# Folded router weights, ScalarE statistics, and the first layer's modulation steps ahead of its output projection

## The chip, the cores and the metric

The kernel runs on one core of one Trainium2 chip. The core has a matrix engine (TensorE, PE in the profile), VectorE (DVE), ScalarE (ACT), GpSimd (POOL) and SyncE (SP), which here only issues transfers; the engines run side by side, each through a queue of its own in order, and wait for one another by semaphores. The metric is the device time of one execution in microseconds (us), as the median of several runs.

## What is computed

Two layers over 256 latent tokens and 256 context tokens of width 1024. In each layer a modulation vector of 6 x 1024 numbers is computed for either kind of token, four mixers and a gated merge give the first update, a router and 16 experts the second. The output is the latent stream, so the second layer treats the context only as far as the latent tokens need it.

```python
def modulate(x, shift, scale):
    return layer_norm(x) * (1 + scale) + shift
...
for l in range(DEPTH):
    mod_lat = jnp.split((jax.nn.silu(c) @ w_mod[l] + b_mod[l])[:, None, :], 6, axis=-1)
    ...
    y_lat = token_mix_out(p_lat, o_lat, *mix_w)
    h_lat = affine_ln(DN_ALPHA * h_lat + mod_lat[2] * y_lat, ln1_g[l], ln1_b[l])
    m_lat = hier_moe(modulate(h_lat, mod_lat[3], mod_lat[4]), *moe_w)
    h_lat = affine_ln(DN_ALPHA * h_lat + mod_lat[5] * m_lat, ln2_g[l], ln2_b[l])
```

`token_mix_out` merges four branches (gated DeltaNet, conformer, Fourier, spatial gating unit), each by its projection and a sigmoid gate, and multiplies the sum with `w_out`. `hier_moe` computes 4 group logits and 16 expert logits per token (20 columns together), takes the best group, the best two of its four experts and weights for both, and adds up two gated MLPs with 512 hidden units.

## The kernel before

**Tiles.** Tokens lie in tiles of 128: layer 0 has four (0 and 1 latent, 2 and 3 context), layer 1 two. A large product is made in three matmuls on halves of each number (`mm3`): `split` turns a loaded weight tile `w` (128 x 512) into a high part `wh` on ScalarE and a low part `wl` on VectorE, and TensorE multiplies high by high, low by high and high by low into PSUM (`psmm`). The tiles rotate through rings of buffers, five of them named `w`. A weight is asked for on SyncE's queue, whose transfers start in order, each as soon as the buffer that it fills is free; GpSimd's queue carries token rows, the scratch tensor `h2s` and gathers.

**Order.** The functions emit the work, and a list scheduler then puts the instructions of each engine in an order by priorities and dependences. Program order is thus near the order of the code without being equal to it, and the instructions of one function can stand among those of another. An engine doesn't leave this order while it runs.

**Mixers and merges of a layer.** `conf_in`, `sgu` and `rms_z` project the normed input, and `merge` is called once for each mixer. It runs over eight output blocks `dt` of 128 channels: a gate projection, the branch's projection, the gated sum on VectorE, and `self.pump(1)` at the end unless the branch is the conformer's (i = 1).

**Modulation steps.** `mod_steps` is a generator over three banks b of a layer (shift and scale of the first norm; gate and shift; scale and gate, as 2 x 1024 numbers for each kind of token). A step asks SyncE for two tiles of 512 KB of `in_wmod_dram` into the ring `w` and multiplies them with the conditioning vectors `silc` into a PSUM bank `psg`; two or eight tiles of weights later `mod_rows` adds the bias, sends the rows to DRAM (`mods`), and transposes those of banks 0 and 1 into `modT`, so that they lie along the partitions. `pump(n)` takes n steps. In layer 0, 24 of 32 steps (banks 1 and 2 of layer 0, banks 0 and 2 of layer 1) are taken in `merge`; of the other eight, `mix_out` takes four, `moe` and later code the rest, with `pump(9)` at the start of `moe`.

**Output projection and its tail.** `mix_out` loads `h` (the residual), splits the merged tensor, and for each pair of tiles s runs `wout(s)`, eight blocks of `w_out`, whose result is scaled by the gate on ScalarE (`yT`). In `norms(tt)` TensorE transposes a tile's result back, VectorE adds it to the residual, takes the statistics (`bn_stats` on two halves, `bn_aggr`, a root on ScalarE, a reciprocal), and applies the first norm with two `scalar_tensor_tensor` operations, giving `h`; then it does the same once more with the modulation rows, giving `xm`, which GpSimd's queue writes to `h2s`. In `logits(tt)` TensorE transposes `xm`, ScalarE copies that to `h2Tt`, and 8 matmuls with the router weights `rw` give 20 columns of `plog` (in the trace each of these stands as two). `route` adds the bias and takes the group maximum `gmx`; a long chain of small VectorE operations follows (`route`, `rank`, up to `mxi`, the largest excess), from whose result the indices `ix` for the gather of the tokens of the first expert come. By "tail" the prediction means the stretch from the first sum of residual and projection to `gmx`. In layer 0 the pair of tiles 2 and 3 comes first (s = 1), then tiles 0 and 1.

## Time and profile before

| | |
|---|---|
| median of 3 runs (lowest, highest) | 1875.15 us (1873.21, 1880.23) |
| profiled execution: its own time, its span | 1878.1 us, 1876.3 us |
| TensorE busy | 1721.4 us, 92% |
| VectorE busy | 1208.7 us, 64% |
| ScalarE busy | 848.3 us, 45% |
| GpSimd busy | 222.4 us, 12% |
| mean granted clock of TensorE, as a share of full speed | 0.953 |
| moved by transfers | 396.50 MB, mean 211 GB/s |

The profile shows one execution. Its span runs from the first to the last instruction that it records, and the execution's own time is 1.8 us longer. The busy shares are means over the whole span; the granted clock is the rate at which TensorE was allowed to run, 1 standing for 2.4 GHz and 0.5 for 1.2 GHz.

### The profile page before, as it was taken

The numbers are of one execution on the slowest core, as the hardware profiler recorded it, in microseconds if no ns is written. First come the engines' busy times: TensorE is split into PE (matmuls) and PEld (weight loads), VectorE is DVE, ScalarE is ACT, GpSimd is POOL, SyncE is SP. The second block draws the span as 40 slices with busy tenths as digits, with TensorE's granted clock in tenths as the row PEclk, the third lists the DMA queues.
The fourth block names the chain that finished last, engine by engine and source line by source line (L and its number), as shares of the span: only waits on it lengthen the run. The fifth ranks groups of instructions, "written<-read, shape, count | busy, mean of one in ns | idle before, by whom it ended". The sixth has DMA issues, their size and how long they took to land. (4 is left out here: it accounts for less than half of the span.)

```text
span 1876.3 us, 31714 instructions
## 1 busy us (share of the span) xinstructions
PE 1721.4 (92%) x11399; PEld 1274.5 (68%) x11399; DVE 1208.7 (64%) x2631; ACT 848.3 (45%) x1688; POOL 222.4 (12%) x321
## 2 busy tenths in 40 slices
PE   7999999998999999699999959989998996799994
PEld 2777777786777788377666516787898996566541
DVE  5878597397353457698575487698678676556203
ACT  3544552343233345187565435445555562355211
POOL 1011101000000205111111021110010010111110
PEclk8999999999999999899999978999999997899997
DMA  8321004523535845889999882222144585799994
GB/s 333 98 75 46 13 24 161 193 88 123 172 125 189 315 144 187 293 309 397 388 379 382 328 309 71 73 82 67 46 136 148 167 318 187 290 414 411 403 410 159
DMA packets 112732, 396.50 MB, mean 211 GB/s; under 512 B 16256, under 2 KB 16352, under 8 KB 112560
## 3 DMA queue, kind: packets, MB, share of 16 engines
q1 hardware_dynamic: 99120, 359.87, 52.6%
q0 software_dynamic: 13440, 34.44, 5.2%
q8 instruction: 94, 1.54, 0.3%
q14 instruction: 78, 0.64, 0.1%
HBM read 388.43 MB, written 17.35 MB: 216 GB/s over the span
## 5 line engine op out<-in xcount | busy, mean ns | idle before, releaser
L266 ACT ACTIVATE wh<-w 128x512 fp32r<-128x512 f32 x500 | 310.1, 630 | 418.4 <-PE psmm L257 299.6
L263 DVE TENSOR_TENSOR wl<-w,wh 128x512 fp32r<-128x512 f32 x484 | 333.6, 701 | 190.1 <-ACT wh L266 184.2
L257 PE MATMUL psmm<-xh,wh 128*128 128x256 f32 (+1 forms) x1280 | 442.3, 346 | 1.2 <-ACT wh L266 1.2
L257 PE MATMUL psmm<-xh,wl 128*128 128x256 f32 (+1 forms) x1280 | 437.7, 342 | 3.9 <-POOL wl L263 3.0
L257 PE MATMUL psmm<-xl,wh 128*128 128x256 f32 (+1 forms) x1280 | 434.5, 340 | 2.2 <-DVE xl L263 2.2
L257 PEld LDWEIGHTS psmm<-xh,wh 128*128 128x128 f32 x1280 | 244.7, 191 | 52.5 <-issue 16.0
L257 PEld LDWEIGHTS psmm<-xh,wl 128*128 128x128 f32 x1280 | 244.3, 191 | 39.4 <-issue 6.5
L257 PEld LDWEIGHTS psmm<-xl,wh 128*128 128x128 f32 x1280 | 244.8, 191 | 31.0 <-issue 3.3
L977 DVE SCALAR_TENSOR_TENSOR cx<-cbuf,part,cx 128x512 f32<-128x512 f32 (+1 forms) x240 | 142.9, 613 | 2.1
L257 PE MATMUL psmm<-br,wh 128*128 128x512 f32 (+1 forms) x512 | 127.7, 336 | 0.4 <-ACT cth L266 0.4
L263 DVE TENSOR_TENSOR hid<-hid,psmm 128x256 f32<-128x256 f32 (+1 forms) x32 | 17.2, 537 | 136.1 <-PE psmm L257 121.2
L257 PEld LDWEIGHTS psmm<-br,wh 128*128 128x128 f32 x512 | 87.4, 188 | 11.7 <-ACT cth L266 0.6
L263 DVE TENSOR_TENSOR xh<-w,xh 128x512 fp32r<-128x512 f32 x124 | 80.7, 686 | 19.1 <-ACT xh L266 17.1
L257 PE MATMUL psmm<-br,wl 128*128 128x512 f32 (+1 forms) x256 | 86.5, 338 | 1.1 <-DVE wl L263 1.1
L257 PE MATMUL psmm<-xh,xTh 128*128 128x512 f32 x224 | 80.0, 415 | 5.7 <-ACT xh L266 5.1
L266 ACT ACTIVATE xh<-w 128x512 fp32r<-128x512 f32 x124 | 72.2, 627 | 19.7 <-DMA w<-in_expert_w_gate_dram 7.2
L257 PE MATMUL psg<-w,silc 128*32 128x512 f32 x320 | 64.5, 657 | 15.5 <-DMA w<-in_wmod_dram 15.5
L257 PE MATMUL psmm<-w,xTh 128*64 128x256 f32 x560 | 67.6, 387 | 1.6 <-DMA w<-in_expert_w_up_dram 1.1
L266 ACT ACTIVATE ye<-psmm,m 128x512 f32<-128x512 f32 x46 | 30.3, 684 | 72.7 <-PE psmm L257 72.3
L257 PEld LDWEIGHTS psmm<-w,xTh 128*64 128x64 f32 x560 | 41.0, 139 | 26.6 <-issue 5.1
L257 PEld LDWEIGHTS psmm<-xh,xTh 128*128 128x128 f32 x224 | 41.3, 190 | 24.6 <-ACT xh L266 9.7
L266 ACT ACTIVATE xTh<-psg 128x512 fp32r<-128x512 f32 (+1 forms) x46 | 26.3, 597 | 63.2 <-PE psg L260 61.5
(474 smaller groups left out, 2847.3 us busy)
## 6 DMA issues: line engine op xcount, KB each, us to landing
w<-in_wch_dram SPq DMA_DIRECT2D x136, 512.0 KB
w<-in_wmod_dram SPq DMA_DIRECT2D x80, 512.0 KB
w<-in_expert_w_down_dram SPq DMA_DIRECT2D x77, 512.0 KB
w<-in_expert_w_gate_dram SPq DMA_DIRECT2D x76, 512.0 KB
w<-in_expert_w_up_dram SPq DMA_DIRECT2D x71, 512.0 KB
w<-in_wbr_dram SPq DMA_DIRECT2D x32, 512.0 KB
xl<-in_expert_w_up_dram SPq DMA_DIRECT2D x28, 512.0 KB
xl<-in_expert_w_gate_dram SPq DMA_DIRECT2D x26, 512.0 KB
```

The source lines that it names most:

```text
L257: self.nc.tensor.matmul(out, lhsT, rhs, start=start, stop=stop, **k)
L263: (eng or self.nc.vector).tensor_tensor(out, a, b, op)
L266: self.nc.scalar.activation(out, in_, func, **k)
L977: nc.vector.scalar_tensor_tensor(x, w, dw[:, c, k:k + 1], x, op0=ALU.mult, op1=ALU.add)
```

## The change

Four edits go together.

- **Router fold.** The logits are no longer a product of the modulated token with the router weights. `router_fold` makes, for each kind of token, weights `scale * rw` with the mean over the 1024 inputs subtracted from each of the 20 columns, and a constant row `c` from the shift and the bias. Then `logits` transposes `h`, not `xm`, and a `scalar_tensor_tensor` on VectorE multiplies the result by the reciprocal deviation `rs` and adds `c`. The folds are made at `dt == 5` of the last gated merge that takes steps (i = 0). `mod_rows` transposes bank 2 as well, since the fold needs the scale along the partitions.
- **Statistics on ScalarE.** The last pair of tiles (0 and 1) goes through `norms_last`. Tile 0's first norm keeps `bn_stats`; tile 1's first norm and the second norm of both get their mean and squares from `norm_sums`, two ScalarE passes over 1024 columns that add up their elements. The rows `xm` are then made by `modulate`, beside the logits.
- **Steps.** `pump(1)` is added in `rms_z` (4 times), in `conf_in` for c > 1 (2) and in `sgu` (4), for layer 0 only. With the 24 of the merges that is more than the generator has, so all 32 steps are taken before `mix_out`, and the calls in `mix_out` and later find none.
- **Small ones.** The factor `ALPHA` of the residual moves into the scale of the projection and into the epsilon of the first norm (`epsa`), and a constant of the ranking is replaced by a comparison.

```diff
+    def norm_sums(self, src, u, eps, junk):
+        rs, st, nm = (self.sb([P, w], f"{n}{u}") for w, n in ((1, "lrs"), (4, "lst"), (2, "lnm")))
+        self.act(junk, src, AF.Identity, accum_out=st[:, 0:1])
+        self.act(nm[:, 1:2], st[:, 0:1], AF.Identity, scale=-1.0 / D)
+        self.act(junk, src, AF.Square, bias=nm[:, 1:2], accum_out=st[:, 2:3])
+        self.act(rs, st[:, 2:3], AF.Sqrt, bias=eps, scale=1.0 / D)
+        self.nc.vector.reciprocal(rs, rs)
+        return nm[:, 1:2], rs
...
     def mod_rows(self, l, b, hfs, rows, bm, pt, mt):
...
-        if b == 2:
-            return
...
-            for m in ((0, 1), (0,))[b]:
+            for m in ((0, 1), (0, 1), (0,))[b]:
...
     def rms_z(self, l, nt):
...
         for hd in range(4):
+            if l == 0:
+                self.pump(1)
...
     def conf_in(self, l, nt, cs):
...
         for c in cs:
+            if l == 0 and c > 1:
+                self.pump(1)
...
     def sgu(self, l, nt):
...
             u = gelu(c)
+            if l == 0:
+                self.pump(1)
...
     def merge(self, l, i, br, nt, first):
...
             if i != 1:
                 self.pump(1)
+            if i == 0 and dt == 5:
+                self.fold = {s: self.router_fold(l, s) for s in reversed(range(nt // 256))}
...
+    def router_fold(self, l, s):
...
+        self.tt(tv, rw, shift[:, :, None].to_broadcast([P, KD, 20]))
+        nc.vector.tensor_reduce(part[:, 0], tv.rearrange("p k n -> p n k"), AX.X, ALU.add)
+        self.tt(w, rw, scale[:, :, None].to_broadcast([P, KD, 20]))
+        nc.vector.tensor_reduce(part[:, 1], w.rearrange("p k n -> p n k"), AX.X, ALU.add)
+        pt = self.ps()
+        self.mm(pt[:, 0:40], self.ones, t[:, 160:200], True, True)
+        self.tt(c, pt[:, 0:20], self.rb, ALU.add)
+        nc.vector.scalar_tensor_tensor(w, pt[:, None, 20:40].to_broadcast([P, KD, 20]), -1.0 / D, w, op0=ALU.mult, op1=ALU.add)
+        return w, c
...
     def mix_out(self, l, ntt):
...
-                nc.vector.scalar_tensor_tensor(x[:, c], h1[:, c], ALPHA, pt, op0=ALU.mult, op1=ALU.add)
-            self.norm_affine(h1, x, g1, b1, f"a{tt % 2}")
+                self.tt(x[:, c], h1[:, c], pt, ALU.add)
...
+        def norms_last():
+            x0, x1 = self.sb([P, D], "xm"), self.sb([P, D], "xm")
...
+                    self.tt(x[:, c], self.h[:, tt, c], pt, ALU.add)
+            mu, rs = self.norm_stats(x0, "a0", self.epsa)
+            nm1, rs1 = self.norm_sums(x1, 0, self.epsa, self.h[:, 1])
+            nc.vector.scalar_tensor_tensor(x0, x0, mu, g1, op0=ALU.subtract, op1=ALU.mult)
+            nc.vector.scalar_tensor_tensor(self.h[:, 0], x0, rs, b1, op0=ALU.mult, op1=ALU.add)
+            nc.vector.scalar_tensor_tensor(x1, x1, nm1, g1, op0=ALU.add, op1=ALU.mult)
+            nc.vector.scalar_tensor_tensor(self.h[:, 1], x1, rs1, b1, op0=ALU.mult, op1=ALU.add)
+            return [(x, *self.norm_sums(self.h[:, tt], tt, self.eps, x), ALU.add) for tt, x in enumerate((x0, x1))]
...
-                    self.tr(pt[:, 128 * k:128 * k + 128], x[:, 512 * q + 128 * k:512 * q + 128 * k + 128])
+                    self.tr(pt[:, 128 * k:128 * k + 128], self.h[:, tt, 512 * q + 128 * k:512 * q + 128 * k + 128])
...
+            nc.vector.scalar_tensor_tensor(self.lg[:, tt], plog[:, 20 * tt:20 * tt + 20], rs, c, op0=ALU.mult, op1=ALU.add)
...
         for tt in range(2, ntt):
-            logits(tt, xs[tt])
+            logits(tt, xs[tt][2])
         self.pump(1)
-        logits(0, xs[0])
-        logits(1, xs[1])
+        for tt in (0, 1):
+            modulate(tt, *xs[tt])
+        for tt in (0, 1):
+            logits(tt, xs[tt][2])
         self.pump(3)
```

How the order of the instructions moves is shown at three places; the numbers behind the names tell one buffer from another.

**ScalarE, tail of layer 1.** `yT` is the scaled projection, `a0brs` to `b1brs` are roots for the two norms of tiles 0 and 1, `h2Tt` are copies for the router. Before, from the last copy of the projection but one:

```order
L266 ACTIVATE yT_17299<-psmm_17563,ys_3247_17288,ys_3246_17287 128x256
L266 ACT_TABLE_LOAD
L266 ACTIVATE a0brs_17604<-a0bag_17603,eps_69 128x1
L266 ACTIVATE a1brs_17638<-a1bag_17637,eps_69 128x1
L266 ACTIVATE b0brs_17614<-b0bag_17613,eps_69 128x1
L266 ACTIVATE h2Tt_17657<-psmm_17658 128x512
L266 ACTIVATE h2Tt_17657<-psmm_17664 128x512
L266 ACTIVATE b1brs_17648<-b1bag_17647,eps_69 128x1
```

After, up to the first such copy, `lst` and `lnm` being the sums and negated means of `norm_sums`:

```order
L265 ACTIVATE yT_17354<-psmm_17619,ys_3260_17343,ys_3259_17342 128x256
L265 ACTIVATE h_17321,lst_3326_17680<-xm_17646 128x1024
L265 ACTIVATE lnm_3327_17681<-lst_3326_17680 128x1
L265 ACTIVATE h_17321,lst_3326_17680<-xm_17646,lnm_3327_17681 128x1024
L265 ACT_TABLE_LOAD
L265 ACTIVATE a0brs_17673<-a0bag_17672,epsa_71 128x1
L265 ACTIVATE lrs_3325_17679<-lst_3326_17680,epsa_71 128x1
L265 ACTIVATE xm_17645,lst_3329_17692<-h_17321 128x1024
L265 ACTIVATE lnm_3330_17693<-lst_3329_17692 128x1
L265 ACTIVATE h2Tt_17713<-psmm_17714 128x512
```

Three passes over 1024 columns and two one-column operations now stand between the projection and the first copy for the router, and the table load stands behind the second of the passes.

**VectorE, tail of layer 1.** Before, from the second norm of tile 0 to that of tile 1:

```order
L448 SCALAR_TENSOR_TENSOR xm_17589<-h_17266,b0bag_17613,rowt_3251_17297 128x1024
L432 RECIPROCAL a1brs_17638<-a1brs_17638 128x1
L449 SCALAR_TENSOR_TENSOR xm_17589<-xm_17589,b0brs_17614,rowt_3250_17295 128x1024
L449 SCALAR_TENSOR_TENSOR h_17266<-xm_17623,a1brs_17638,rowt_3249_17293 128x1024
L428 BN_STATS b1bst_17646<-h_17266 128x6
L429 BN_STATS b1bst_17646<-h_17266 128x6
L430 BN_AGGR b1bag_17647<-b1bst_17646 128x2
L448 SCALAR_TENSOR_TENSOR xm_17623<-h_17266,b1bag_17647,rowt_3251_17297 128x1024
L432 RECIPROCAL b1brs_17648<-b1brs_17648 128x1
L449 SCALAR_TENSOR_TENSOR xm_17623<-xm_17623,b1brs_17648,rowt_3250_17295 128x1024
```

After, from the first norm of tile 1 to the second norm of both (`lg` are the logits):

```order
L1271 SCALAR_TENSOR_TENSOR xm_17646<-xm_17646,lnm_3327_17681,rowt_3261_17346 128x1024
L432 RECIPROCAL a0brs_17673<-a0brs_17673 128x1
L1270 SCALAR_TENSOR_TENSOR h_17321<-xm_17645,a0brs_17673,rowt_3262_17348 128x1024
L441 RECIPROCAL lrs_3325_17679<-lrs_3325_17679 128x1
L1272 SCALAR_TENSOR_TENSOR h_17321<-xm_17646,lrs_3325_17679,rowt_3262_17348 128x1024
L1277 SCALAR_TENSOR_TENSOR xm_17645<-h_17321,lnm_3330_17693,rowt_3264_17352 128x1024
L441 RECIPROCAL lrs_3328_17691<-lrs_3328_17691 128x1
L1278 SCALAR_TENSOR_TENSOR xm_17645<-xm_17645,lrs_3328_17691,rowt_3263_17350 128x1024
L1291 SCALAR_TENSOR_TENSOR lg_17356<-psg_17355,lrs_3328_17691,rwc_3127_16695 128x20
L1277 SCALAR_TENSOR_TENSOR xm_17646<-h_17321,lnm_3333_17701,rowt_3264_17352 128x1024
L441 RECIPROCAL lrs_3331_17699<-lrs_3331_17699 128x1
L1278 SCALAR_TENSOR_TENSOR xm_17646<-xm_17646,lrs_3331_17699,rowt_3263_17350 128x1024
```

The statistics of `h` by `bn_stats` are gone; the second norm's products of tile 0 are followed by its logits, and those of tile 1 stand behind them.

**TensorE, last part of the spatial gating unit of layer 0.** `wsT` are the gating weights, `vln` the normed values, `xh` and `wh` halves of the projection. Before, three tiles of modulation weights (`w`, `silc`) lie ahead of the first gating product:

```order
L257 MATMUL psmm_4084<-xh_137,wl_4081 128x512
L260 MATMUL psmm_4112<-ident_77,ca_4061 128x128 x4
L257 MATMUL psg_4235<-w_4236,silc_66 32x512 x2
L257 MATMUL psg_4235<-w_4238,silc_66 32x512 x2
L257 MATMUL psg_4235<-w_4303,silc_66 32x512 x2
L257 MATMUL psmm_4136<-wsT_3697,vln_4111 128x128
```

After, from the second tile ahead of the transposes of `ca`:

```order
L256 MATMUL psmm_4142<-xh_139,wl_4139 128x512
L256 MATMUL psg_3558<-w_4169,silc_66 32x512 x2
L256 MATMUL psg_3558<-w_4171,silc_66 32x512 x2
L259 MATMUL psmm_4178<-ident_79,ca_4119 128x128 x4
L256 MATMUL psg_3558<-w_4288,silc_66 32x512 x2
L256 MATMUL psg_3558<-w_4290,silc_66 32x512 x2
L256 MATMUL psmm_4202<-wsT_3731,vln_4177 128x128
```

Two steps (four tiles) now stand about the transposes, two tiles ahead of them and two behind.

## Rows read from the trace of the kernel before

**Rows 1.** Busy time by stretch: stretch, its length, then by engine, clock, DMA share.

```profile
290.00:690.00 400.00, 392.73 (x1804) 300.20 (x1803) 222.22 (x404) 134.98 (x230) 28.90 (x39) 0.99 0.51 173
748.00:777.00 29.00, 26.14 (x170) 15.02 (x168) 19.99 (x37) 7.26 (x16) 1.11 (x2) 0.94 0.94 341
794.00:1087.00 293.00, 280.34 (x1440) 189.96 (x1440) 200.54 (x418) 183.65 (x329) 37.73 (x42) 0.97 0.94 360
1566.00:1589.20 23.20, 11.68 (x57) 10.80 (x55) 17.50 (x29) 4.43 (x9) 1.08 (x2) 0.63 0.57 226
1603.00:1830.00 227.00, 216.10 (x1336) 128.74 (x1337) 93.30 (x228) 85.73 (x157) 31.76 (x32) 0.99 1.01 398
```

**Rows 2.** Timeline of VectorE, tail of layer 0: start, duration, instruction, idle time before.

```profile
748.18 0.69 DVE L1213 SCALAR_TENSOR_TENSOR xm<-h,psmm 128x512 f32<-128x512 f32 x1 [0.82 <-PE psmm L260]
...
776.90 0.17 DVE L1265 TENSOR_REDUCE gmx<-lg 128x4 f32<-128x16 f32 x1
...
787.39 0.69 DVE L263 TENSOR_TENSOR mt<-psg,mt 128x512 f32<-128x512 f32 x1
...
788.52 0.13 DVE L1318 TENSOR_SCALAR mxi<-mx 128x1 int32<-128x1 f32 x1
```

**Rows 3.** Timeline of VectorE, tail of layer 1.

```profile
1565.54 1.28 DVE L1213 SCALAR_TENSOR_TENSOR xm<-h,psmm 128x512 f32<-128x512 f32 x2 [4.85 <-PE psmm L260]
...
1569.20 1.28 DVE L448 SCALAR_TENSOR_TENSOR xm<-xm,a0bag,rowt 128x1024 f32<-128x1024 f32 x1
...
1570.39 0.16 DVE L432 RECIPROCAL a0brs<-a0brs 128x1 f32<-128x1 f32 x1
...
1589.39 0.16 DVE L1265 TENSOR_REDUCE gmx<-lg 128x2 f32<-128x8 f32 x1
```

**Rows 4.** Timeline of TensorE, tail of layer 0 to the first expert.

```profile
761.81 1.05 PE L257 MATMUL psg<-w,silc 128*32 128x512 f32 x4 [1.80 <-DMA w<-in_wmod_dram]
...
774.63 1.96 PE L257 MATMUL psg<-rw,h2Tt 128*128 128x20 f32 x16
...
794.08 1.94 PE L260 MATMUL psg<-ident,xe 128*128 128x128 f32 x8 [10.17 <-DVE sp_a L624]
```

**Rows 5.** Groups of ScalarE by form: busy us, mean ns of one, idle before.

```profile
L266 ACT ACTIVATE w<-h,m1nm,m1brs 128x1024 f32<-128x1024 f32 x2 | 2.5, 1234 | 1.7 <-DVE m1nm L442 1.7
```

**Rows 6.** Timeline of ScalarE, mixers of layer 0 and start of its experts.

```profile
369.99 0.67 ACT L266 ACTIVATE ca<-psmm,part 128x512 f32<-128x512 f32 x1
...
375.49 0.67 ACT L266 ACTIVATE cth<-psmm,hbg 128x512 f32<-128x512 f32 x1
...
488.50 0.63 ACT L266 ACTIVATE wh<-w 128x512 fp32r<-128x512 f32 x1 [4.67 <-DMA w<-in_wch_dram]
...
793.47 1.28 ACT L1360 ACT_TABLE_LOAD   x1 [11.71 <-ACTq L1611]
...
794.77 0.22 ACT L1360 ACTIVATE gex<-gex 128x16 f32<-128x16 f32 x1
```

**Rows 7.** Timeline of TensorE, router matmuls in the tail of layer 1.

```profile
1578.27 1.94 PE L260 MATMUL psmm<-ident,xm 128*128 128x128 f32 x8 [11.34 <-DVE xm L449]
...
1585.52 3.60 PE L257 MATMUL psg<-rw,h2Tt 128*128 128x20 f32 x16
```

**Rows 8.** Timeline of TensorE, mixers of layer 0.

```profile
343.54 1.06 PE L257 MATMUL psg<-w,silc 128*32 128x512 f32 x8
...
443.19 0.79 PE L257 MATMUL psmm<-wsT,vln 128*128 128x128 f32 x2 [4.47 <-ACT vln L266]
...
531.01 1.08 PE L260 MATMUL psg<-ident,vo 128*128 128x128 f32 x2 [2.26 <-DVE vo L263]
```

**Rows 9.** The tile `h2s`: time from issue to landing of its transfers.

```profile
DMA to landing us min/median/max: 3.5/6.4/7.6
```

**Rows 10.** Timeline of GpSimd: the first gather of expert tokens in layer 0.

```profile
785.47 1.57 POOL L1483 DMA_INDIRECT xe<-h2s,ix  x1 [13.91 <-DVE rt L1309]
```

**Rows 11.** Timeline of SyncE's queue: the weights of a conformer projection.

```profile
484.82 0.33 SPq L318 DMA_DIRECT2D w<-in_wch_dram  x1
```

More of the change, by code (lines that the diff above doesn't have):

```diff
@@ L276, in setup @@
         nc.vector.memset(self.eps, EPS)
+        self.epsa = self.sb([P, 1], "epsa")
+        nc.vector.memset(self.epsa, EPS / ALPHA ** 2)
         self.mhalf = self.sb([P, 1], "mhalf")
@@ L1166, in row @@
         return t
+    def router_fold(self, l, s):
+        nc = self.nc
+        rw = self.rw.rearrange("p (k n) -> p k n", k=KD)
+        shift, scale = self.modT[l][:, 3, :, s], self.modT[l][:, 4, :, s]
+        w = self.sb([P, KD, 20], "rwf") if s else rw
+        c = self.sb([P, 20], f"rwc{s}")
+        t = self.sb([P, 512], "ev")
+        part = t[:, 160:200].rearrange("p (i n) -> p i n", i=2)
+        tv = t[:, 0:160].rearrange("p (k n) -> p k n", k=KD)
+        self.tt(tv, rw, shift[:, :, None].to_broadcast([P, KD, 20]))
[7 more added lines that the diff above has]
+        return w, c
     def mix_out(self, l, ntt):
@@ L1185, in mix_out @@
         m2 = self.modT[l][:, 2]
-        nc.vector.tensor_scalar(s1, m2, 0.5, None, op0=ALU.mult)
-        self.tt(s2, m2, self.pp("b_out")[:, :, None].to_broadcast([P, KD, 2]))
+        nc.vector.tensor_scalar(s1, m2, 0.5 / ALPHA, None, op0=ALU.mult)
+        nc.vector.scalar_tensor_tensor(s2, m2, 1.0 / ALPHA, self.pp("b_out")[:, :, None].to_broadcast([P, KD, 2]), op0=ALU.mult, op1=ALU.mult)
         g1, b1 = self.row(l, "big", 0, 0), self.row(l, "big", 1, 0)
@@ L1212, in norms, with modulate, logits @@
                 c = slice(512 * q, 512 * q + 512)
-                nc.vector.scalar_tensor_tensor(x[:, c], h1[:, c], ALPHA, pt, op0=ALU.mult, op1=ALU.add)
-            self.norm_affine(h1, x, g1, b1, f"a{tt % 2}")
+                self.tt(x[:, c], h1[:, c], pt, ALU.add)
+            mu, rs = self.norm_stats(x, f"a{tt % 2}", self.epsa)
+            nc.vector.scalar_tensor_tensor(x, x, mu, g1, op0=ALU.subtract, op1=ALU.mult)
+            nc.vector.scalar_tensor_tensor(h1, x, rs, b1, op0=ALU.mult, op1=ALU.add)
+            mu, rs = self.norm_stats(h1, f"b{tt % 2}")
+            return x, mu, rs, ALU.subtract
+        def norms_last():
+            x0, x1 = self.sb([P, D], "xm"), self.sb([P, D], "xm")
+            for tt, x in enumerate((x0, x1)):
+                for q in range(2):
+                    pt = self.ps()
+                    for k in range(4):
+                        self.tr(pt[:, 128 * k:128 * k + 128], yT[:, 4 * q + k, 128 * tt:128 * tt + 128])
+                    c = slice(512 * q, 512 * q + 512)
+                    self.tt(x[:, c], self.h[:, tt, c], pt, ALU.add)
[6 more added lines that the diff above has]
+            return [(x, *self.norm_sums(self.h[:, tt], tt, self.eps, x), ALU.add) for tt, x in enumerate((x0, x1))]
+        def modulate(tt, x, mu, rs, op):
             m3, m4 = ms[tt // 2]
-            self.norm_affine(x, h1, m4, m3, f"b{tt % 2}", x)
+            nc.vector.scalar_tensor_tensor(x, self.h[:, tt], mu, m4, op0=op, op1=ALU.mult)
+            nc.vector.scalar_tensor_tensor(x, x, rs, m3, op0=ALU.mult, op1=ALU.add)
             nc.gpsimd.dma_start(self.h2s[128 * tt:128 * tt + 128, :], x)
-            return x
-        def logits(tt, x):
+        def logits(tt, rs):
+            rw, c = fold[tt // 2]
             hT = self.sb([P, KD, P], "h2Tt")
```

36 lines of the change are left out of this document (20 added, 16 removed).

## Prediction

> **What bounds the kernel now.** First view: busy time by stretch [rows 1]. From 290 to 690 us (mixers and merges of layer 0) TensorE is busy 392.73 of 400 us, so a matmul added there lengthens the kernel. From 794 us (experts of layer 0) it is busy 280 of 293 us; from 1603 us (experts of layer 1) the DMA share is 1.01. Both are blocks that end sooner by as much as they start sooner. Between them lie the tails of the two output projections, 748 to 777 and 1566 to 1589.2 us: there TensorE is busy 26.1 of 29 us with a granted clock of 0.94 (modulation steps fill it), and 11.7 of 23.2 us with 0.63, a mean of its levels 2.4 and 1.2 GHz.
>
> Second view: the timeline of VectorE in both tails. From the first sum of residual and projection to the router's first maximum (gmx), layer 0 takes 776.90 - 748.18 = 28.7 us [rows 2], layer 1 takes 1589.39 - 1565.54 = 23.9 us [rows 3]. Layer 0 is longer although TensorE runs faster there: its in-order queue holds modulation steps that wait for their weights (1.80 us at 761.81 [rows 4]) ahead of the router's transposes, and ScalarE, which copies these, stands behind them. So a tail is a chain over three engines, and its length is what the change can win.
>
> **Prices.** On VectorE a 512-wide sum costs 0.60 us from start to start (two end after 1.28 [rows 3]), and I give a half of bn_stats the same; a 1024-wide scalar_tensor_tensor costs 1570.39 - 1569.20 = 1.19 [rows 3]. On ScalarE a 1024-wide pass costs 1.23 [rows 5], a 512-wide one 0.63, a one-column operation about 0.22, a table load 1.28 [rows 6]. On TensorE the router matmuls of one tile take 1.96 us in the first tail [rows 4] and 3.60 in the second, eight transposes there 1.94 [rows 7]: 1.2 GHz, after 11.34 us without work.
>
> No row shows a ScalarE pass that also adds up its elements. Lower bound: the plain pass, 1.23. Upper bound: one more smallest operation each, 1.23 + 0.22 = 1.45. I take 1.23: that row reads and writes as many elements.
>
> **Moved steps: +8 us.** Eight steps (24 are done ahead of the projection before, 32 now) leave the tail and the routing of layer 0 for the stretch where TensorE has no room. One takes 1.06 us [rows 8], of which I count 0.98, since the next matmul overlaps its end: 7.8. Three more groups of four transposes fall there (two are new, for the bank of the second scale; one is moved): a quarter of 1.94 each at 2.4 GHz [rows 7], 1.5. The two folds add two 40-column matmuls, estimated at 0.2 each. Sum 9.7. Two waits can take some of it: 4.47 us at 443.19 and 2.26 at 531.01 [rows 8]. The first is the way of the last SGU channel over VectorE, GpSimd and ScalarE; steps fill part of it already, and in the new order one step and not one and a half follows its transposes, so it shrinks little. The second gains one step ahead of it. I count 1.5. Bounds: 9.7 with none hidden, 9.7 - 6.7 = 3.0 with both waits filled. I take 8, since the order puts most steps between projections, where nothing waits. The folds' VectorE work (seven small operations each) lies in a stretch with VectorE busy 222 of 400 us [rows 1]; without that cover it would be about 2 us per fold. The moved DMAs, 16 tiles of 512 KB on SyncE's queue, meet a DMA share of 0.51 [rows 1].
>
> **Tail of layer 0: -11 us.** The new order from 748.18. VectorE: four sums and one weight split to 751.2, bn_stats of tile 0 to 752.4. It then waits for the logits of tile 2, whose copies on ScalarE stand behind four weight splits: about 754.0. Then tile 0's aggregate, a split, its root (754.9), its first product (756.1), the logits of tile 3 (756.7), h of tile 0 (757.9), tile 1's product (759.1), a split, h of tile 1 (760.9). ScalarE goes on in order: sum of h0 from 757.9 to 759.2, two copies and the mean to 760.5, squares to 761.7, sum of h1 to 762.9, two one-column operations and a copy to 763.9, squares to 765.1, copy 765.7, root 766.0. VectorE modulates tile 0 to 765.0 and the first half of tile 1 to 766.2, takes logits 0, ends tile 1 at 767.5 and takes logits 1: gmx at 767.7, 9.2 us sooner than 776.90. From there to the largest excess (mxi) it took 788.52 - 776.90 = 11.6 us [rows 2], and the experts start at 794.08 [rows 4]. In it two weight splits and the last bank's sum (787.39 [rows 2]) are gone, 3 x 0.60: 1.8. Together 11. Bounds: 9.2 + 1.8 + 2.5 = 13.5 if VectorE never waited (its own operations sum to 17.0 us); 5 if each pass costs 1.45, TensorE falls to 1.2 GHz once it has no steps, and the first copies come 3 us late.
>
> A transfer nearly comes next: tile 1 is written back from 767.6 and lands 6.4 us later, at most 7.6 [rows 9]: 774.0 to 775.2. The gather that reads it left at 785.47 [rows 10], 8.6 us after gmx, one split of which is gone: 775.7. It stays covered by 0.5 to 1.7 us.
>
> **Tail of layer 1: -4.5 us.** Tile 1's sum is ready at 1565.54 + 4 x 0.60 = 1568.0. ScalarE then has in a row: sum, mean, squares, the table load for the root (before, it lay in idle time), two roots: to 1572.6. VectorE has finished statistics and both products at 1571.8, waits for the root, writes h0 at 1573.8 and h1 at 1575.0. ScalarE: sum of h0, mean, copy, squares, sum of h1, root, mean, copy, squares, copy, root, copy: 4 x 1.23 + 4 x 0.60 + 4 x 0.22, less some 0.2 where they overlap: to 1581.7. TensorE has 3.60 us of logits per tile at 1.2 GHz and ends tile 1's about 1584.8; gmx at 1585.0 against 1589.39. At 2.4 GHz 1583. With passes at 1.45: 1586.4. I take 4.5.
>
> On the table load the Trainium skill ("ScalarE: Activation LUTs", section "What ACT_TABLE_LOAD costs") gives 1.28 us plus a drain of 1.38. The trace shows the 1.28, and the next operation starts 0.02 us behind it [rows 6]. By the page layer 1 would gain 3.1 instead of 4.5, and the kernel would take 1869.
>
> **Small edits, nothing.** ALPHA folded into the projection's scale, the other epsilon, the constant made on the spot: one operation stands for another.
>
> **Sum.** 8 - 11 - 4.5 = -7.5. The profiled execution took 1878.1 us (1876.3 and 1.8 around it), 2.95 above the median 1875.15. So 1870.6 for it, 1867.7 at the median.
>
> **Rivals.** *More hides (0.22).* Both waits in the mixers fill (3 instead of 8) and TensorE keeps 2.4 GHz in layer 1 (6.5): 3 - 11 - 6.5 = -14.5, 1860.7. For it: 6.7 us of waits lie in the way of the moved steps. Against it: nothing is added that keeps TensorE busy in layer 1. *ScalarE is the new bound (0.14).* Every summing pass at its upper price costs 6 x 0.22 in each layer, 2.6, and the loss of the steps puts layer 0's router matmuls and transposes at 1.2 GHz, 3 us: -2, 1873.2. For it: VectorE waits for ScalarE three times in the new chain, and the two tails differ in clock as their steps do, 0.94 and 0.63 [rows 1]. Beside this the Trainium skill ("TensorE: Matmul & The Clock Gate", section "What's actually happening") has half rate as the default that activity releases; the two tails agree. *The weight ring stalls, slower (0.09).* Five tiles rotate through the ring `w`. In the z projections steps now take two of every three, and SyncE can ask for a projection's weights only once the step before the last projection is consumed. A tile needs 488.50 - 484.82 = 3.7 us to land [rows 6, 11] and two splits, 1.3: 5.0, against a projection of 375.49 - 369.99 = 5.5 [rows 6] and a step of 1.0 ahead of it. Cover 1.5. With 7.6 us, the longest landing of as large a transfer [rows 9], TensorE idles 2.4 per projection: over the ten that get a step 24 us, +16.5, 1891.7. It decides from 1.7 us a projection. Against it: in the merges, which rotate the same ring with steps, TensorE shows no wait for weights.
>
> **Numbers.** My forecast has 0.55, with -3 to -11.5, that is 1864 to 1872. 0.5% is 9.4 us here, about what a measurement of this kernel tells from no change. Faster by more: the first rival and the forecast's edge, 0.33; slower: the last rival without its mild end, 0.07; within: 0.60. The range reaches from the first rival to just above no change: 1861 to 1877.
>
> **What would show it.** Right: in layer 0 gmx about 19.5 us after the first sum and the experts 11 us sooner against it, in layer 1 19.5 us; the mixers 8 us longer without a wait of TensorE for weights; ScalarE passes of 1.2 to 1.3 us. Wrong: passes of 1.5 us or more, a wait of TensorE for `w`, waits at 443 and 531 that are gone, or experts that wait for the gather.

## The result, and the profile after

The changed kernel takes 1892.7 us (median of 8 runs, 1886.68 to 1896.55) against 1876.41 us before in the same series (8 runs): a ratio of 1.0077, 95% interval 1.0056 to 1.0099, so about 14.4 us more (10.5 to 18.6). The forecast was 7.5 us less. The profiled execution took 1896.55 us (span 1894.8), the one before 1878.1, so the two traces stand 18.45 us apart.

Busy time of the changed kernel by stretch, columns as in [rows 1]; the stretches run from matmul to matmul as 290 to 690 us did, and from the first sum to `gmx` in both tails:

```profile
291.85:711.81 419.96, 408.02 (x1884) 302.81 (x1883) 227.45 (x429) 134.22 (x230) 28.52 (x38) 0.99 0.53 185
769.51:792.54 23.03, 18.06 (x108) 16.48 (x106) 17.62 (x29) 14.76 (x33) 1.10 (x2) 0.69 0.70 271
1585.82:1605.64 19.82, 12.08 (x60) 11.16 (x58) 14.92 (x21) 11.53 (x25) 1.07 (x2) 0.62 0.62 240
```

What was 400.2 us of mixers (290.26 to 690.44) is 420.0. The first tail is 23.0 us long instead of 28.7 [rows 2], the second 19.8 instead of 23.9 [rows 3]. Both tails got shorter; the mixers lost over twice what was forecast.

TensorE's timeline in the mixers of layer 0, where it stood idle, and one row each of the first tail and of layer 1's merge (start, duration, instruction, idle time before and what ended it):

```profile
485.67 0.66 PE L259 MATMUL psmm<-ident,mt 128*128 128x128 f32 x4 [0.97 <-DVE mt L397]
...
624.13 0.42 PE L256 MATMUL psmm<-ev,ones 128*128 128x40 f32 x2 [0.92 <-DVE ev L1197]
626.46 0.39 PE L256 MATMUL psmm<-ev,ones 128*128 128x40 f32 x2 [1.91 <-DVE ev L1197]
...
639.75 0.63 PE L259 MATMUL psmm<-ident,mt 128*128 128x128 f32 x4 [2.92 <-DVE mt L397]
...
788.65 3.57 PE L256 MATMUL psg<-rw,h2Tt 128*128 128x20 f32 x16 [2.58 <-DVE lg L1291]
```

The first four rows are new: twice TensorE stands in front of the matmul of a fold's column sums (`ev`), which VectorE has not finished, twice in front of the transposes of the second scale's rows (`mt`), 6.7 us together. None of its waits between 292 and 711 us ends with a weight tile `w`. The last row is new too: tile 1's router matmuls wait until VectorE has read tile 0's logits (`lg`).

VectorE in between, in the second fold (one of the two):

```profile
625.14 0.41 DVE L1195 TENSOR_REDUCE ev<-ev 128x20 f32<-128x160 f32 x1
625.47 0.32 DVE L262 TENSOR_TENSOR rw<-rw,modT 128x160 f32<-128x160 f32 x1
625.70 0.30 DVE L1014 BATCH_NORM_STATS2 cst<-psmm 128x6 f32<-128x128 f32 x1
625.91 0.41 DVE L1197 TENSOR_REDUCE ev<-rw 128x20 f32<-128x160 f32 x1
```

The sums end at 626.32, with an operation of the conformer among them; TensorE has had the matmul next in line since 624.55.

ScalarE at the start of the experts of layer 0:

```profile
810.18 0.20 ACT L1430 ACTIVATE re<-re 128x4 f32<-128x4 f32 x1
815.78 0.21 ACT L265 ACTIVATE ea<-rowt 128x8 f32<-128x8 f32 x1 [5.39 <-DMA rowt<-in_rows_dram]
815.89 1.07 ACT L265 ACTIVATE xTh<-psg 128x512 fp32r<-128x512 f32 x2
```

GpSimd's loads of parameters for layer 1:

```profile
803.66 0.62 POOL L1790 DMA_DIRECT2D part<-in_part_dram  x1
809.84 0.58 POOL L1792 DMA_DIRECT2D rowt<-in_rows_dram  x1 [5.56 <-DMA rowt<-mods]
```

The copies `xTh` of the first expert's second half stand behind `ea`, a small operation of layer 1 on parameter rows that have not landed. The load of these rows (`rowt`, the second row above) left 2.1 us after the expert's first transposes at 807.72, behind the end of a branch that GpSimd passes only then. In the kernel before it left at 793.14, 0.9 us ahead of them [rows 4]: there both loads stand behind the branch, and it is passed sooner.

ScalarE's new passes in layer 1, in order of time:

```profile
1588.33 1.06 ACT L265 ACTIVATE h<-xm 128x1024 f32<-128x1024 f32 x1 [2.39 <-DVE xm L262]
1589.30 0.19 ACT L265 ACTIVATION_READ_ACCUMULATOR h<-xm 128x1 f32 x1
1589.51 0.20 ACT L265 ACTIVATE lnm<-lst 128x1 f32<-128x1 f32 x1
1589.75 1.15 ACT L265 ACTIVATE h<-xm,lnm 128x1024 f32<-128x1024 f32 x1
1590.80 0.19 ACT L265 ACTIVATION_READ_ACCUMULATOR h<-xm,lnm 128x1 f32 x1
1591.01 1.28 ACT L265 ACT_TABLE_LOAD   x1
1592.30 0.29 ACT L265 ACTIVATE a0brs<-a0bag,epsa 128x1 f32<-128x1 f32 x1
```

A summing pass takes 1589.51 - 1588.33 = 1.18 and 1.26 us with the reading of its sum: the lower bound of the prediction, 1.23, held. On the table load the Trainium skill ("ScalarE: Activation LUTs", "What ACT_TABLE_LOAD costs") adds a drain of 1.38 us; the trace does not agree, the next operation stands 0.01 us behind the load's end.

### The profile page after: what moved, and what is told of

It reads as the page before. It is cut to its first block, busy times and chain, and to the rows that moved or that the text cites. A ratio compares the mean times of both kernels' runs of the same rounds, so it can differ in the third digit from the quotient of the medians.

```text
span 1894.8 us, 31801 instructions
## 1 busy us (share of the span) xinstructions
PE 1731.6 (91%) x11413; PEld 1277.5 (67%) x11413; DVE 1206.6 (64%) x2644; ACT 859.7 (45%) x1718; POOL 221.6 (12%) x321
## 5 line engine op out<-in xcount | busy, mean ns | idle before, releaser
L256 PE MATMUL psg<-w,silc 128*32 128x512 f32 x320 | 57.6, 647 | 13.0 <-DMA w<-in_wmod_dram 13.0
L256 PEld LDWEIGHTS psmm<-xh,xTh 128*128 128x128 f32 x224 | 41.9, 194 | 26.9 <-ACT xh L265 9.8
L256 PEld LDWEIGHTS psmm<-w,xTh 128*64 128x64 f32 x560 | 41.5, 141 | 27.5 <-issue 6.4
```

The costliest lines, as they stand in the source:

```text
L256: self.nc.tensor.matmul(out, lhsT, rhs, start=start, stop=stop, **k)
```

## Experiments

In this table each time is the difference of two starts in the trace of that kernel, in us. *Mixers*: from VectorE's eighth sum into `merged` to ScalarE's first `yT`. *Tail 1*, *tail 2*: first sum to `gmx`. *Expert*: first sum to TensorE's first transposes `xe` in layer 0. *Light*: from there to the first matmul `psmm<-merged,xTh`, with which the experts with few tokens (the light ones) start. The ratio is to the kernel before in the same job, with its 95% interval. A trace is one execution: e5 and e6, which run the two kernels with nothing but their tiles moved, differ from them by 1.4 and 2.3 us in the mixers and by 1.0 and 2.5 in *light*, so smaller differences in these two columns tell little; their tails agree within 0.1.

| kernel | mixers | tail 1 | expert | light | tail 2 | ratio |
|---|---|---|---|---|---|---|
| before | 375.6 | 28.7 | 45.9 | 57.5 | 23.9 | 1 |
| changed | 395.1 | 23.0 | 38.2 | 62.0 | 19.8 | 1.0077 (1.0056 to 1.0099) |
| e1 no extra steps | 381.3 | 22.9 | 41.5 | 59.3 | 19.8 | 1.0020 (0.9992 to 1.0048) |
| e2 steps alone | 382.3 | 26.2 | 41.3 | 58.5 | 23.8 | 1.0008 (0.9982 to 1.0035) |
| e3 VectorE statistics | 394.3 | 23.1 | 39.1 | 58.9 | 19.1 | 1.0088 (1.0054 to 1.0123) |
| e4 no fold | 384.7 | 26.2 | 41.6 | 58.5 | 24.7 | 1.0074 (1.0045 to 1.0102) |
| e5 before, shifted | 374.2 | 28.7 | 45.7 | 56.5 | 23.9 | 1.0020 (0.9992 to 1.0047) |
| e6 changed, shifted | 397.4 | 23.0 | 37.9 | 59.5 | 19.8 | 1.0105 (1.0069 to 1.0141) |
| e7 late fold | 392.1 | 23.0 | 38.1 | 60.1 | 19.8 | 1.0075 (1.0047 to 1.0103) |
| e8 rows first | 395.0 | 23.0 | 38.4 | 56.6 | 19.8 | 1.0078 (1.0052 to 1.0104) |
| e9 operands apart | 378.5 | 28.7 | 45.4 | 56.6 | 23.8 | 1.0038 (1.0012 to 1.0064) |
| e10 fold alone | 375.9 | 26.9 | 46.4 | 58.9 | 19.1 | 0.9983 (0.9964 to 1.0002) |
| e11 fold, statistics | 375.9 | 22.5 | 39.0 | 58.8 | 19.8 | 0.9975 (0.9952 to 0.9998) |
| e12 all, mended | 387.9 | 23.0 | 38.5 | 56.7 | 19.8 | 1.0021 (1.0003 to 1.0039) |
| e13 mended, two logs | 388.1 | 20.4 | 35.2 | 58.5 | 19.2 | 1.0000 (0.9982 to 1.0019) |
| e14 e11 with two logs | 375.8 | 20.9 | 39.0 | 59.4 | 19.2 | 0.9962 (0.9946 to 0.9978) |
| e15 steps in ranking | 377.2 | 21.2 | 61.1 | 58.0 | 19.8 | 1.0069 (1.0044 to 1.0093) |

**One part undone, or one alone.** e1 takes the extra steps out (in `conf_in`, `sgu` and `rms_z` alike); e2 is the reverse, on the kernel before:

```diff
-            if l == 0:
-                self.pump(1)
```

e3 calls `norms` for the last pair:

```diff
-        xs[0], xs[1] = norms_last()
+        xs[0], xs[1] = norms(0), norms(1)
```

e4 gives the router the modulated rows and its own weights, and leaves out the transposes of the second scale's bank:

```diff
-            if i == 0 and dt == 5:
-                self.fold = {s: self.router_fold(l, s) for s in reversed(range(nt // 256))}
...
-                    self.tr(pt[:, 128 * k:128 * k + 128], self.h[:, tt, 512 * q + 128 * k:512 * q + 128 * k + 128])
+                    self.tr(pt[:, 128 * k:128 * k + 128], x[:, 512 * q + 128 * k:512 * q + 128 * k + 128])
```

> The changed kernel without its ten extra steps ahead of the output projection (24 of 32 ahead, as before); fold and ScalarE statistics stay. Main theory (the eight moved steps are paid in full on TensorE, 8.2 us in the trace, and they also bring the load of layer 1's parameter tile ahead of a branch, where GpSimd waits for it, 4.4 us at the first expert of layer 0): the mixers of layer 0 get 8 to 9 us shorter than in the changed kernel and ScalarE's 5.4 us wait for the parameter rows before the first expert is gone; the steps come back to the first tail and cost 2 to 6 us there; 1881 to 1886 against 1892.7. Rival (TensorE's matmuls run 1 to 2% slower in the changed program whatever the steps do, 229 against 233 ns from start to start): not below 1887, and matmuls from start to start still 233 ns or more.

> The kernel before with the ten extra steps alone: no fold, no ScalarE statistics. Main theory: 8 to 9 us more in the mixers, 4.4 us more at the first expert of layer 0 (the parameter load stands ahead of the branch here too), less what the first tail gains without steps among its router work (28.7 us before, 4 to 8 us shorter): 1880 to 1886, slower than before by 4 to 10. Rival (steps are nearly free, and the fold makes the loss): within 3 us of before, 1873 to 1879.

> The changed kernel with the last pair's statistics on VectorE again (the same form as the pair before it), all else changed. Main theory: ScalarE's passes were worth about half of what both tails gained; each tail gets 2 to 4 us longer, so 1896 to 1901. Rival (ScalarE is the new bound of the tails, its two passes per norm cost more than the two halves of bn_stats): the tails get shorter, 1886 to 1891.

> The changed kernel without the router fold and without the transposes of the second bank that it needs: the router works on the modulated rows again, after both modulation products of a tile; the extra steps and the ScalarE statistics stay. Main theory: TensorE's waits for the fold's sums (0.92 and 1.91 us) and for the rows of the second bank (0.97 and 2.92 us) go, and 2 us of its own work, so the mixers get 8 to 9 us shorter than in the changed kernel; the tails get 2 to 5 us longer each, since the router now waits for the modulation: 1888 to 1892. Rival (the fold's waits are hidden by other slack of the mixers): mixers within 3 us of the changed kernel and 1897 to 1903.

e1: without the extra steps the mixers are 13.7 us shorter, more than the 8 to 9 expected, since the new waits shrink with them (0.54 us for rows and 0.93 for a fold instead of 6.7), and the first tail is no longer than with them: with the fold and the ScalarE statistics, steps in the tail cost nothing up to `gmx`. The first expert comes 3.3 us later against the first sum, though. The matmuls keep the slower pace of the changed kernel (below). Its ratio is 3.8 us above before, which its interval does not tell from no change, its median 1880.59 us just below the main theory's range. e2: 6.7 us more in the mixers, 4.6 us less to the first expert (2.5 of them in the tail), no measurable difference in all; on its ratio the rival's "nearly free" holds, because the way to the first expert gave most of the steps' cost back. e3: beside the extra steps the ScalarE statistics were worth 0.1 us in the first tail and -0.7 in the second, so neither theory holds; at 1893.64 us it has the changed kernel's time, with slower projections in layer 1 (below). e4: without the fold the mixers are 10.4 us shorter and the tails 3.2 and 4.8 us longer, and its median of 1890.85 us lies in the main theory's range. Of the 10.4 us, 6.7 are the four waits and 1.4 the fold's own matmuls and transposes. Part of the rest is the clock: right behind the fold's waits, from 628.18 to 631.58 us, the changed kernel's granted clock is 0.51 and eight projection matmuls start 0.43 instead of 0.23 us apart, 1.6 us in all. So the fold is what shortens the second tail, and the first once steps are out of it; made where it is, it also costs the mixers most.

**Where the operands lie.** A slower pace of matmuls showed in stretches that no part of the change touches. In the merge of layer 0 a projection, a branch's projection and a step follow each other without idle time; the steps that bound such a block, in the changed kernel and in e12 and e9 below:

```profile
297.96 1.06 PE L256 MATMUL psg<-w,silc 128*32 128x512 f32 x8
...
307.50 1.06 PE L256 MATMUL psg<-w,silc 128*32 128x512 f32 x8
```

```profile
301.67 1.07 PE L256 MATMUL psg<-w,silc 128*32 128x512 f32 x8
...
311.11 1.06 PE L256 MATMUL psg<-w,silc 128*32 128x512 f32 x8
```

```profile
302.05 1.07 PE L257 MATMUL psg<-w,silc 128*32 128x512 f32 x8
...
311.59 0.64 PE L257 MATMUL psg<-w,silc 128*32 128x512 f32 x4
```

The block takes 9.54, 9.44 and 9.54 us, at the same granted clock of 1. e5 moves all tiles by 32 bytes with one unused tile ahead of them (e6 by 96, with 24 numbers in it):

```diff
         nc.vector.memset(self.eps, EPS)
+        self.pad = self.sb([P, 8], "pad")
+        nc.vector.memset(self.pad, 0.0)
```

e9 moves the inputs of the projections (`xh`, `xl`) alone against the weights (`wh`, `wl`):

```diff
         self.h = self.sb([P, 4, D], "h")
+        if l == 0:
+            self.gap = self.sb([P, 16], "gap")
+            nc.vector.memset(self.gap, 0.0)
```

> The kernel before with one unused tile of 32 bytes per partition put ahead of its data (and one operation that clears it), so that all later tiles lie 32 bytes further in SBUF, with the same offsets within 128 bytes as in the changed kernel; nothing else. Theory (the pace of the projections' matmuls follows from where their operands lie: 229 to 230 ns from start to start of 512-wide ones in the kernel before and in the steps alone, whose tiles lie alike, 233 in the changed kernel and in the one without extra steps): 512-wide projections at 233 ns, 256-wide ones near 122 instead of 125 ns, so layer 0's mixers and earlier stages 6 us longer, layer 1's 4 us shorter, 1876 to 1884. Rival (the pace belongs to the changed program's order or to the execution): 229 to 230 ns as before.

> The changed kernel with one unused tile of 96 bytes per partition ahead of its data, which gives its tiles the offsets within 128 bytes that they have in the kernel before; nothing else. Theory (place decides the pace): 512-wide projections back at 229 to 230 ns, 256-wide ones at 125, layer 0's mixers 4 us shorter and the whole within 6 us of the changed kernel, 1886 to 1893. Rival (order or execution decides): 233 ns as in the changed kernel.

> The kernel before with one unused tile of 64 bytes per partition between the rings of the split weights and the split inputs of the projections, so that these two lie 39296 and not 39232 bytes apart; the weights stay where they were. Theory (the pace of the projections' matmuls follows from the distance between their two operands modulo 256 bytes: 64 in the kernel before and in both kernels of it at 229 to 230 ns for 512 columns and 124 to 126 for 256; 192 in the changed kernel and in all of it at 233 and 120 to 124; 128 in the two at 232.4 and 125 to 128): 512-wide ones at 232.4 ns, 256-wide ones 2 ns slower, 8 to 10 us more, 1884 to 1888. Rival (chance or the order of the program): 229 to 230 ns and no change.

The first theory fell: e5 stayed at 9.45 us and e6 at 9.54, wherever the tiles lay. What e5 and e6 leave alone is the distance of the two operands (39232 bytes before, 40128 in the changed kernel, by the addresses in the two programs), and e9, which changes only that, went from 9.45 to 9.54, with 2.9 us more in the mixers and a ratio of 1.0038, 7.1 us where 8 to 10 were expected. In all 17 traces the block takes 9.44 to 9.46 us where `xh` and `wh` lie 64 bytes apart modulo 256, and 9.53 or 9.54 where it is 128 or 192. The 256-wide projections of layer 1 differ too, but not by this rule alone: from the first to the eighth `yT` of the output projection it takes 18.49 us before, 17.77 in the changed kernel, in e1 and in e5 to e8, 18.6 to 18.9 in e3, e4 and e9. Why is not settled.

**The incidental waits.** e7 emits the fold's matmuls later (`fold_end` is the second half of `router_fold`) and adds the 1 to the bias:

```diff
-            if i == 0 and dt == 5:
-                self.fold = {s: self.router_fold(l, s) for s in reversed(range(nt // 256))}
+            if i == 0 and dt == 4:
+                made = {s: self.router_fold(l, s) for s in reversed(range(nt // 256))}
+            if i == 0 and dt == 7:
+                self.fold = {s: self.fold_end(*made[s]) for s in made}
```

e8 changes the order of four loads:

```diff
-        self.part = self.sb([P, NP_], "part")
-        load(self.part, self.a["part"][l])
         self.rowt = self.sb([P, NR_], "rowt")
...
         load(self.rb, self.a["rb"][l].partition_broadcast(P))
+        self.part = self.sb([P, NP_], "part")
+        load(self.part, self.a["part"][l])
```

> The changed kernel with the fold's matmuls emitted three blocks of the merge after its VectorE sums, and with the 1 of the scale added to the bias ahead of the steps' last sum rather than to the finished rows: the same work, but TensorE no longer has it next in line while VectorE makes it. Theory (TensorE's in-order queue stood 0.9 and 1.9 us for the fold's sums and 1.0 and 2.9 us for the scale rows in layer 0, 2.4 us in layer 1): these five waits shrink to under 1 us together, 7 to 9 us gained, 1884 to 1887. Rival (something else in the merge ends as late, so the waits only move): 1890 to 1894.

> The changed kernel with the four loads of layer 1's small parameters in another order: the broadcast rows first, the large parameter tile last; so the rows' load stands ahead of the branch behind the ranking and the large one behind it. Theory (in the changed kernel GpSimd starts the rows' load only after its branch, which waits for the large tile's landing, and ScalarE's operation on the rows, 5.4 us late, holds the copies of the first expert's tokens): ScalarE's wait is under 1 us and the first experts start 3 to 5 us sooner, 1888 to 1890. Rival (the experts of layer 0 wait for their weights or gathers anyway): second expert's copies no sooner, 1892 to 1893.

e7: both waits for the fold in layer 0 and the one in layer 1 (2.43 us at 1519.60 in the changed kernel) are gone, as is the first for the rows; the second stayed. TensorE's timeline of e7 there:

```profile
640.35 0.51 PE L259 MATMUL psmm<-ident,mt 128*128 128x128 f32 x2 [2.78 <-DVE mt L262]
```

The mixers gained 3.0 us and those of layer 1 2.7, 5.7 of the expected 7 to 9; the median of 1891.31 us, with runs from 1877 to 1896, does not show it. e8: ScalarE no longer waits, as its timeline says:

```profile
809.96 0.20 ACT L1430 ACTIVATE re<-re 128x4 f32<-128x4 f32 x1
810.05 0.20 ACT L265 ACTIVATE ea<-rowt 128x8 f32<-128x8 f32 x1
811.26 1.23 ACT L265 ACTIVATE xTh<-psg 128x512 fp32r<-128x512 f32 x2 [1.01 <-PE psg L259]
```

The stretch to the light experts is 5.4 us shorter than in the changed kernel, which had it 4.5 us longer than the kernel before; the ratio, 1.0078 against 1.0077, shows none of it. The stretch in the changed kernel, before and in e8 (columns as in [rows 1]):

```profile
807.72:869.73 62.01, 59.23 (x285) 46.09 (x287) 55.37 (x143) 49.71 (x88) 8.46 (x12) 0.91 0.76 268
```

```profile
794.08:851.58 57.50, 56.70 (x284) 44.76 (x286) 55.16 (x139) 50.14 (x88) 7.22 (x11) 0.94 0.86 302
```

```profile
807.49:864.12 56.63, 55.87 (x285) 43.95 (x287) 55.30 (x139) 50.29 (x88) 8.58 (x12) 0.96 0.82 297
```

TensorE stands idle for 2.8 us in the changed kernel and 0.8 in the other two, so 2.0 us are the late load. The rest is the same matmuls at a lower granted clock. How much of that the wait caused is not shown: in e13 below ScalarE does not wait either, and the stretch takes 58.5 us at a clock of 0.93. One thing of the theory was wrong: GpSimd's next load left only at 809.07 here too, with the small rows ahead of the branch, so what it waits for there is not the large tile's landing. It matters only which load stands ahead.

**Versions put together.** e10 to e12 carry e7's edits and the operands 64 bytes apart modulo 256; e10 has no extra steps and VectorE statistics, e11 no extra steps, e12 all parts and e8's order.

> The router fold alone: no extra steps, statistics on VectorE; the fold's matmuls emitted three merge blocks after its sums, the 1 of the scale added to the bias, and the split inputs set 64 bytes modulo 256 from the weights as in the kernel before (one unused tile). Theory (of the three parts the fold alone gains: 3 to 6 us in the first tail and 4 to 5 in the second, against 2 to 3 us in the mixers): 5 to 9 us under the kernel before of the same job. Rival (what the tails gain is lost again before the experts, as part of it was in the changed kernel): within 3 us of before.

> The same with the statistics of the last pair on ScalarE as in the changed kernel (no extra steps, late fold, operands as before). Theory (two ScalarE passes and their small operations take as long on the path as bn_stats on VectorE): within 2 us of the fold alone. Rival (they free VectorE): 3 to 6 us under the fold alone.

> All parts of the change with the incidental losses mended: extra steps, fold and ScalarE statistics, but late fold matmuls, the 1 in the bias, the rows' load ahead of the large one, and operands as before. Theory (the eight steps are paid in full, 8 us, and bring nothing once the fold has taken the router off the modulation): 6 to 10 us above the fold with statistics. Rival (the steps pay in the first tail once the waits are gone): not above it.

The fold costs the mixers nothing measurable once it is late (375.9 against 375.6 us) and shortens the second tail by 4.8 us; in the first it gains 1.9 up to `gmx` and loses that before the first expert. Alone its ratio puts it 3.2 us under the kernel before, with an interval that includes no change (6.8 under to 0.4 above); its median is 0.3 us under, so the rival stands. The statistics on ScalarE gain 4.4 us in the first tail when steps are in it; a likely reason, not tested by itself, is that they take work from the queue in which the steps' sums stand. In the medians that is 3.2 us, beyond the expected 2, but the two intervals overlap. The first tail is 26.9 us with the fold alone, 23.1 with the steps out as well (e3), 22.5 with ScalarE statistics instead (e11) and 23.0 with both: the two parts gain the same microseconds, and only the steps have a price in the mixers. e12 against e11 is the price of the extra steps: 12.0 us in the mixers, 0.5 us returned by the first expert, 8.7 us in the medians, as the theory said. Of the 12.0, TensorE is busy with steps for 8.7 (32.59 against 23.86 us), and 2.8 are the second wait for the scale's rows, which e12 still has at 636.22 us. Against the changed kernel e12 shows that the incidental losses were real though neither e7 nor e8 moved the whole: 1.0003 to 1.0039 against 1.0056 to 1.0099.

**What ends the first tail.** e13 and e14 give e12 and e11 two PSUM tiles for the logits of a pair:

```diff
-        plog = self.ps("g")
+        plogs = [self.ps("g"), self.ps("g")]
...
             rw, c = fold[tt // 2]
+            plog = plogs[tt % 2]
```

e15 is e11 with its eight late steps all emitted behind the ranking:

```diff
-        self.pump(1)
...
-        self.pump(3)
```

> The mended kernel with all parts (extra steps, late fold, ScalarE statistics, rows' load first, operands as before), and the router logits of a pair's two tiles in two PSUM tiles instead of one. Theory (in the changed kernel and in the mended one TensorE waits 2.58 us in the first tail and 0.42 in the second with tile 1's router matmuls until VectorE, behind two modulation operations, has read tile 0's logits out of the same PSUM tile): both waits are gone, the first tail is 2 to 3 us shorter than 23.0. Rival (the copies on ScalarE or the clock of 1.2 GHz end the tail anyway): within 0.5 us.

> The fold with statistics on ScalarE and no extra steps (operands as before), and the logits of a pair in two PSUM tiles. Theory: the tails of 22.5 and 19.8 us get at most 0.5 us shorter each, since steps filled the wait in the first and it was 0.4 us in the second; within 2 us of the same kernel with one PSUM tile. Rival (the wait was hidden under the steps and ends the tail): 2 us or more.

> The fold with statistics on ScalarE, no extra steps ahead of the projection, and none in the tail either: the eight steps of layer 0 that are left are emitted behind the router's ranking. Theory (TensorE and VectorE's queue are free of them in the tail, and the ranking has 10 us in which TensorE has no work): first tail as short as with all steps ahead, 22 to 23 us, and the first expert no later than in the kernel that keeps four of them in the tail. Rival (their eight megabytes now come when the experts' weights are loaded, and the first expert waits for either): the first expert of layer 0 starts 2 to 8 us later against the first sum.

e13's TensorE in the first tail, the second pair of rows being tile 1's:

```profile
774.85 3.60 PE L256 MATMUL psg<-rw,h2Tt 128*128 128x20 f32 x16
778.28 1.95 PE L259 MATMUL psmm<-ident,h 128*128 128x128 f32 x8
780.06 3.60 PE L256 MATMUL psg<-rw,h2Tt 128*128 128x20 f32 x16
```

No wait is left, and the tail is 20.4 us: 2.7 us shorter, the whole of the wait. e14 won 1.6 us there where at most 0.5 was expected, so the shared tile cost something under the steps too; it has the lowest ratio, 1871.33 us, 7.1 us (4.1 to 10.1) under the kernel before. Against e14, e13 pays 12.3 us in the mixers for the extra steps and has 3.8 back by the first expert, so what steps in the tail cost depends on what else ends the way there: 0.5 us (e11), 3.3 (e1), 3.8 (e14). In e15 the tail is as short as hoped, but the first expert comes 22 us later:

```profile
801.64 3.12 PE L256 MATMUL psg<-w,silc 128*32 128x512 f32 x8 [3.18 <-DMA w<-in_wmod_dram]
...
811.56 0.66 PE L259 MATMUL psg<-ident,xe 128*128 128x128 f32 x2 [5.34 <-DVEq L1680]
```

The steps wait for their tiles until 801.64 and TensorE reaches the expert behind them. The rival held, more strongly than it was put.

## Why the prediction was wrong, step by step

**Moved steps, +8 (mis-sized).** The mixers took 19.5 us more. The work was counted right: TensorE is busy with steps for 31.5 us instead of 23.0 (from the eighth sum to the first `yT`), 8.5 against 7.8, beside 2 us of transposes and folds against 1.9; and e12 against e11 confirms that it is paid in full. The hiding was right too. The waits that the prediction named [rows 8], in the changed kernel:

```profile
453.42 0.49 PE L256 MATMUL psmm<-wsT,vln 128*128 128x128 f32 x2 [4.13 <-ACT vln L265]
...
540.35 0.33 PE L259 MATMUL psg<-ident,vo 128*128 128x128 f32 x1 [0.18 <-DVE vo L262]
540.95 0.33 PE L259 MATMUL psg<-ident,vo 128*128 128x128 f32 x1 [0.27 <-DVE vo L262]
541.55 0.33 PE L259 MATMUL psg<-ident,vo 128*128 128x128 f32 x1 [0.27 <-DVE vo L262]
542.15 0.33 PE L259 MATMUL psg<-ident,vo 128*128 128x128 f32 x1 [0.28 <-DVE vo L262]
```

The one at 443.19 went from 4.47 to 4.13 us, the one of 2.26 at 531.01 became four that sum to 1.0, and one of 0.30 at 429.40 is gone: 1.9 us together against 1.5. What failed is the cover of the folds, which the prediction had priced and then set to nothing: "without that cover it would be about 2 us per fold". A VectorE busy for 222 of 400 us is no cover, since TensorE's queue holds the fold's matmul next and cannot go round it: 2.83 us for the two, and 2.43 in layer 1 (e7). The waits for the second scale's rows, 3.89, were not counted at all. Another 4.1 us, with no term in the sum either, are the pace of the projections, 46 of them at 0.09 us; e12, with the operands 64 bytes apart, has the old pace. 8.5 + 2 - 1.9 + 6.7 + 4.1 = 19.4 of 19.5.

**Tail of layer 0, -11 (mis-sized, and put down to the wrong part).** Up to `gmx` it gained 5.7 instead of 9.2. Of the missing 3.5 us, 2.6 are the wait for `lg` (e13), a wait that took the place of one removed and that the order would have shown: tile 1's matmuls write the PSUM tile that VectorE reads behind two modulations. The rest is near the 1.2 GHz that the bounds had at 3 us: router matmuls of 3.57 and 3.60 us per tile instead of 1.96 [rows 4], granted clock 0.69. The Trainium skill ("TensorE: Matmul & The Clock Gate", "What's actually happening") has half rate as the default that activity releases, and the trace agrees. From `gmx` to the experts 2.0 us were gained, 1.8 forecast. Then 4.5 us were given back between the first expert's transposes and the light experts, a loss without a term in the sum, of which 2.0 are idle time of TensorE behind the late load (e8). And the gain up to `gmx` did not need the moved steps: e1 and e11, which keep four steps in the tail, have 22.9 and 22.5 us.

**Tail of layer 1, -4.5 (right in size).** It gained 4.0, with passes at the lower bound, and the forecast's chain stood in the trace: tile 1's `h` ends 9.7 us behind the first sum (9.5 forecast), its router matmuls 19.5 (19.3). But e10 has 19.1 us with statistics on VectorE, so the fold alone made the gain, and the ScalarE passes took 0.7 us of it back; the prediction did not tell the two apart.

**The rivals.** *More hides*: of the 6.7 us of waits 1.6 went, and the second tail's granted clock stayed at 0.62. *ScalarE is the new bound*: the passes took 1.18 and 1.26 us and not the 1.45 that it rests on; its other half, the first tail's router matmuls at 1.2 GHz, came true. *The weight ring stalls*: the wait for the ring `w` did not come, and that its 1891.7 us is near the time measured is chance. Its 7.6 us for a landing was misread as well: [rows 9] mixes a write of `h2s`, which landed in 3.5 us, with gathers from it, whose median is 7.3.

**Sum.** By the two traces: 1.9 ahead of the mixers, 19.5 mixers, -5.7 and -2.0 first tail and ranking, 4.5 first expert, 2.1 up to the second tail (with the fold's wait of 2.4), -4.0 second tail, 2.2 behind it: 18.5 of 18.45. The 1.9 and the 2.2 have no cause shown: e5 and e10, both at the faster pace, already reach the eighth sum 6.7 us apart.

## What to carry to other kernels

Work that fills a queue beside a latency chain is nearly free there; moved to where its engine is full it is paid in full: here 12 us in the mixers for 0.5 to 3.8 by the first expert. Ask of every matmul that depends on a small computation elsewhere what TensorE has next in line when the scheduler has placed it: emitted three blocks after its sums, the fold cost the mixers nothing measurable. A PSUM tile that two consecutive results share can become a wait when the engine that reads it has other work in front, here 2.6 us.

## Not expected of the hardware

The pace of 512-wide fp32r projections differed by 1%, 9.45 against 9.54 us for one block, with the distance of their two operands in SBUF (e9). And executions differ by a stretch of lower clock: in the trace of before 192.95 us from 1126.45, in that of e2 184.81 us from 1127.37 for the same work (same columns as above):

```profile
1126.45:1319.40 192.95, 181.37 (x1476) 144.76 (x1474) 155.92 (x418) 98.51 (x226) 19.87 (x53) 0.94 0.23 71
```

```profile
1127.37:1312.18 184.81, 171.89 (x1476) 137.60 (x1474) 155.91 (x417) 98.44 (x226) 21.05 (x53) 1.00 0.24 74
```

The granted clock is 0.94 and 1.00. In the 17 traces the same work takes 184.7 to 186.7 us in eight and 190.6 to 194.1 in nine. The changed kernel's trace has 193.1 us there, so this is not in the difference of the two; it is why one execution's total says less than its stages.
